# Splitting one of two fused activation sums by itself in a Strassen-style feed-forward

## The chip, the cores and the metric

The kernel runs on one core of a Trainium2 chip, in one launch. The metric is device time in microseconds (us): the median of repeated runs. A separate profiled execution gives the rows that are read here. Engines: PE (TensorE, matrix products), DVE (VectorE), ACT (ScalarE), POOL (GpSimd), SP (issues DMAs).

## The reference, cut to what matters

Two layers of a streaming encoder run over 1024 prompt tokens and 32 sample tokens (1056 columns together). The change touches only the feed-forward of each layer, D_MODEL = 1024, D_FF = 4096:

```
def channel_and_ple(h, p_i, norm_ffn_w, w_ff1, w_ff2, norm_ple_w, w_ple_gate, w_ple_proj):
    u = rms_norm(h, norm_ffn_w) @ w_ff1
    h = h + jnp.square(jax.nn.relu(u)) @ w_ff2
    ...
```

Everything else (input projections, latent attention, retention, output projection, gated embedding) is as in an ordinary encoder layer and is left out.

## The kernel before, in words

**Numbers.** Every operand of a big product is kept as a pair of 16-bit tiles, a high part and a remainder ("lo"): ACT writes the high part with a copy, DVE or POOL then subtracts it from the 32-bit source and writes the remainder. `split_ops` (around L780) does this for operands of the second half of the feed-forward: one ACT copy, one subtraction. A product is three matmuls for each block of 128 inputs: weight high by operand high, weight high by operand lo, weight lo by operand high.

**Seven products.** Tokens are halved (columns 0 to 527 and 528 to 1055) and features are paired, so that a product is a 2 by 2 block product, done in seven products after Strassen and Winograd. Products are numbered 1 to 7 and issued in the order 1, 7, 6, 4, 5, 2, 3. `PROD` says which of the seven operands (0 to 6) a product reads:

```
PROD = {1: 0, 2: 1, 3: 6, 4: 2, 5: 3, 6: 4, 7: 5}
```

So the second product issued (7) reads operand 5, the third (6) reads operand 4.

**First half** (`ff1_units`). A unit is 264 columns of each half (two units, here u0 and u1, go through each product one after the other: 12 matmuls each) of one pair of feature blocks. In the first two steps of a layer the units are 176 wide and there are three pairs. There are 34 units in each layer, 68 in all. After each product `ff1_chains` starts the work on its result. The four blocks of the activation are y11, y12, y21, y22, and the operands of the second half are 0: y11, 1: y12, 2: y22, 3: s1 = y21 + y22, 4: s2 = s1 - y11, 5: y11 - y21, 6: y12 - s2. The scratch tile Ra of a unit (named `ra` in the trace) has two quarters of the rows read here: `lo` (first) and `up` (second). y21 stands in `up`; y11 stands in PSUM (`u.f`, named `mx`); s1 stands in `rb`; y22 stands in `mm`.

**Where the change is** (`c11`, around L915). After product 2 has given y11, `c11` waits until s1 has been planned, writes y11 - y21 over `up` and s1 - y11 into `lo`, and splits both with one `split_ops` for operands (4, 5): one ACT copy and one subtraction, 528 wide (`r<-ra` on ACT, `r<-ra,r` on DVE or POOL).

**Second half** (`ff2_units`). Four steps of the first half (75 us) are followed by four steps of the second half, and so on, four times in each layer. The first step of the second half begins directly behind product 3 of the last unit. These eight places, where the second half begins, are called crossings 1 to 8 here: crossing 1 begins at about 693.5 us, crossing 2 at 850.5, crossing 3 at 1005.8, crossing 4 at 1159.7; crossings 5 to 8, in the second layer, at 2023.1, 2181.1, 2336.7 and 2490.3. The second half adds each product into h with a DVE instruction (`h<-o,h` and the like).

**Order.** A planner (`Pipe`, `Model`) fixes the order of every engine's instructions when the program is built, by a model of costs. Each chain is a generator: it hands over its next instruction, which is placed when its inputs and its engine are free in the model; among those that can go, first come goes first. A chain that waits for another (`u.has("s1")`) looks again every 0.2 us of model time. The model lets DVE instructions with two SBUF inputs and POOL instructions with SBUF inputs run only one at a time ("port"). `tt` (also inside `split_ops`) lets the planner choose DVE or POOL. On the chip the engines run their queues strictly in this order. At the same time as all this, ACT, DVE and POOL convert the next weights (`w<-s`, `w<-stage`, `w<-t` on ACT and DVE, `t<-stage,s`, `stage<-stage`, `t<-stage,t`, `t<-s,t` on POOL).

Of the kernel before, what the change touches and what calls it, by code (L numbers as in the profile page):

```python
# [15 lines left out]
ALU = mybir.AluOpType  # L16
# [157 lines left out]
def drop(*tiles):  # L174
    for t in tiles:
        if Slots.parts.get(t.name, 0) > 1:
            Slots.parts[t.name] -= 1
            continue
        slots, i = Slots.owner.pop(t.name)
        slots.free.append(i)  # L180
# [212 lines left out]
def kernel(ctx, tc, xT, pT, wts, vecs, qnw, kvnw, cf, ch, cckT, ckrT, st_in,  # L393
# [5 lines left out]
    pipe = Pipe()  # L399
# [61 lines left out]
    def tt(first, *args, bias=0.2, lead=0.3, **kw):  # L461
        other = pool if first is dve else dve
        return Either((first.q.tensor_tensor(*args, lead=lead, **kw), other.q.tensor_tensor(*args, lead=lead, **kw)), bias)

    dve, act, pool = (Engine(e, k, model, keep, ordered)
                      for e, k in ((nc.vector, "dve"), (nc.scalar, "act"), (nc.gpsimd, "pool")))
# [159 lines left out]
    def halves(a):  # L626
        return a.rearrange("p (s t) -> p s t", s=2)
# [124 lines left out]
    def split_ops(op, which, src, a, w, eng):  # L752

        if len(which) == 2:
            sl = op["p"][which]
            hi, lo = sl[:, 0, :, a:a + w], sl[:, 1, :, a:a + w]
        else:
            sl = op["o"][which[0]]
            hi, lo = sl[:, 0, a:a + w], sl[:, 1, a:a + w]
        yield act.q.activation(hi, src, AF.Copy, scale=1.0)  # L760
        yield dve.q.tensor_tensor(lo, src, hi, op=ALU.subtract) if eng is None else tt(eng, lo, src, hi, op=ALU.subtract)
        for o in which:
            op["n"][o].update(range(a // 88, (a + w) // 88))
# [78 lines left out]
    def stt(out, a, s, b, op0=ALU.mult, op1=ALU.add):  # L842
        dve.scalar_tensor_tensor(out, a, s, b, op0=op0, op1=op1)
# [26 lines left out]
    def ff1_chains(u, i, rc):  # L870
        w, op, a, Ra, Rb = u.w, u.op, u.a, u.ra, u.rb
        lo, up = Ra[:, :w], Ra[:, w:2 * w]
        e7, s1 = Rb[:, :w], Rb[:, w:2 * w]
        if i == 1:
            act.activation(lo, u.A[:, :w], AF.Copy, scale=UN)
        elif i == 7:
            act.activation(e7, u.e, AF.Copy, scale=UN)
        elif i == 6:
            act.activation(up, u.A[:, :w], AF.Copy, scale=UN)
        elif i == 4:  # L880
            stt(up, u.e, UN, up)

            def c21():
                yield dve.q.scalar_tensor_tensor(up, up, 0.0, up, op0=ALU.max, op1=ALU.mult)
                u.got.add("y21")
            pipe.spawn(c21())
        elif i == 5:
            stt(u.e, u.A[:, :w], UN, e7)

            def y22():  # L890
                yield from split_ops(op, (2,), u.e, a, w, None)
                yield u.has("s1")
                drop(u.E)

            def c22():
                yield act.q.activation(u.e, u.e, AF.Relu)
                yield act.q.activation(u.e, u.e, AF.Square)
                pipe.spawn(y22())
                yield u.has("y21")
                yield dve.q.tensor_tensor(s1, up, u.e, op=ALU.add)  # L900
                u.got.add("s1")
                yield from split_ops(op, (3,), s1, a, w, dve)
                yield u.has("s2")
                drop(Rb)
            pipe.spawn(c22())
        elif i == 2:
            stt(lo, u.f, UN, lo)
            stt(u.f, lo, 0.0, lo, ALU.max, ALU.mult)

            def y11():  # L910
                yield from split_ops(op, (0,), u.f, a, w, None)
                yield u.has("s2")
                drop(u.F)

            def c11():  # L915
                pipe.spawn(y11())
                yield u.has("s1")
                yield dve.q.tensor_tensor(up, u.f, up, op=ALU.subtract)
                yield dve.q.tensor_tensor(lo, s1, u.f, op=ALU.subtract)
                u.got.add("s2")  # L920
                yield from split_ops(op, (4, 5), halves(Ra[:, :2 * w]), a, w, dve)
                yield u.has("s4")
                drop(Ra)
            pipe.spawn(c11())
        else:
            act.activation(u.A[:, :w], u.A[:, :w], AF.Relu, scale=UN)

            def y12():
                yield from split_ops(op, (1,), u.A[:, :w], a, w, None)
                yield u.has("s4")  # L930
                drop(u.A)

            def c12():
                yield act.q.activation(u.A[:, :w], u.A[:, :w], AF.Square)
                pipe.spawn(y12())
                yield u.has("s2")
                yield dve.q.tensor_tensor(rc, u.A[:, :w], lo, op=ALU.subtract)
                u.got.add("s4")
                yield from split_ops(op, (6,), rc, a, w, pool)
                u.got.add("end")  # L940
            pipe.spawn(c12())

    def ff1_units(*units):
        pipe.wait(lambda: room(2 * len(units) + 1))
        R = T("r")
        for u in units:
            u.ra, u.rb = T("ra"), T("rb")
        for i, name, kind, start in ((1, "A", None, True), (7, "E", "mm", True), (6, "A", None, False), (4, "E", "mm", False),
                                     (5, "A", None, False), (2, "F", "mx", True), (3, "A", None, False)):
            for n, u in enumerate(units):  # L950
                u.prod(i, name, kind, start)
                ff1_chains(u, i, R[:, n * u.w:(n + 1) * u.w])
                pipe.poll()
            seen = []
            for u in units:
                if all(u.W is not x for x in seen):
                    u.done(i)
                    seen.append(u.W)

        def rest():  # L960
            yield lambda: all("end" in u.got for u in units)
            drop(R)
        pipe.spawn(rest())
# [87 lines left out]
    for L in range(DEPTH):  # L1051
# [823 lines left out]
        for e in range(4):  # L1875
# [14 lines left out]
            for z in range(4):  # L1890
                n = 8 * e + 4 + z
                load(n + 1)
                for g in range(1 if n < 31 else 3):
# [6 lines left out]
                    if e == 3 and z == 0 and g == 0:  # L1900
# [13 lines left out]
                        up = Units(upt[i // 2][:, (i % 2) * 1024:(i % 2 + 1) * 1024].rearrange("p (a n) -> p a n", a=2) for i in range(4))  # L1914
# [154 lines left out]
```

## Time and profile before

| what | value |
|---|---|
| median of 3 runs | 2712.25 us (2709.64 to 2714.51) |
| the profiled execution | 2710.96 us, its span 2709.2 us |
| mean granted TensorE clock | 0.974 of full speed |
| PE busy | 2566.6 us, 95% of the span |
| DVE busy | 1866.6 us, 69% |
| ACT busy | 1310.0 us, 48% |
| POOL busy | 1056.2 us, 39% |

The span is what the trace covers; the execution's own time has 1.8 us more around it. Busy shares are means over the whole span: the stretches in which an engine sets the pace are found in the rows of those stretches.

### The profile page before, as it was taken

How to read it: one execution, taken by the hardware profiler on the slowest of the kernel's cores; microseconds unless marked ns; L12 is line 12 of the kernel's file. 1: busy time of each engine (PE TensorE's matmuls, PEld its weight loads, DVE VectorE, ACT ScalarE, POOL GpSimd, SP SyncE). 2: the span in 40 equal slices, each digit the busy share in tenths (PEclk: the TensorE clock that was granted, in tenths of full speed). 3: DMA queues.
4: the chain of work that ended last, by engine and by line, in shares of the span. 5: the costliest groups of instructions: out<-in, count | busy, mean ns of one | idle time of the engine just before them, and what ended most of it. 6: DMA issues, size and time to landing. Idle time of an engine off the chain costs nothing.

```text
span 2709.2 us, 58534 instructions
## 1 busy us (share of the span) xinstructions
PE 2566.6 (95%) x23322; PEld 2006.0 (74%) x23322; DVE 1866.6 (69%) x4555; ACT 1310.0 (48%) x3277; POOL 1056.2 (39%) x1267
## 2 busy tenths in 40 slices
PE   7998989988999999999999989999799999999997
PEld 4765667768888888887656556777688888888965
DVE  6767776656667585875657677775585766768755
ACT  6533366646345262635445344665462534536342
POOL 7123355654333332433331334564732333333331
PEclk8999989989999999999999999999899999999999
DMA  4201010000111212121112011100011111122112
GB/s 136 71 28 49 17 53 27 21 9 33 51 60 52 67 40 75 43 68 50 56 53 70 9 41 34 58 6 29 13 40 50 57 52 59 53 66 68 56 44 64
DMA packets 87057, 130.53 MB, mean 48 GB/s; under 512 B 11584, under 2 KB 36448, under 8 KB 86784
## 3 DMA queue, kind: packets, MB, share of 16 engines
q1 hardware_dynamic: 86496, 126.25, 15.1%
q8 instruction: 182, 2.98, 0.4%
q14 instruction: 91, 0.75, 0.1%
q10 hardware_dynamic: 288, 0.55, 0.1%
HBM read 116.98 MB, written 7.02 MB: 46 GB/s over the span
## 4 chain that ended last, share of the span: by engine, by line
PE 86%; DVE 8%; POOL 3%; ACT 2%; issue 1%; DMA 0%; DVEq 0%; POOLq 0%; ACTq 0%
PE mm L476 33%; PE o L476 20%; PE st L476 19%; PE mx L476 12%; DVE r L285 3%; POOL x L285 1%; PE st L483 1%; PE mx L483 1%; DVE ra L285 1%; DVE w L285 1%; POOL r L285 1%; DVE sf L285 0%; DVE mt L285 0%; PE mm L483 0%; DVE h L285 0%
## 5 line engine op out<-in xcount | busy, mean ns | idle before, releaser
L476 PEld LDWEIGHTS <-w 128*128 128x128 f16 x13176 | 1276.5, 99 | 315.6 <-issue 50.3
L476 PE MATMUL mm<-w,x 128*128 128x256 f16 (+3 forms) x1920 | 334.9, 326 | 11.6 <-DVE sil L285 6.0
L476 PEld LDWEIGHTS <-x 128*128 128x128 f16 x2304 | 222.0, 99 | 147.7 <-DVE sil L285 10.8
L476 PE MATMUL st<-x,w 128*128 128x264 f16 (+2 forms) x1896 | 247.0, 284 | 19.1 <-ACT ra L285 19.1
L285 DVE SCALAR_TENSOR_TENSOR w<-s,w 128x512 f16<-128x512 f32 (+2 forms) x280 | 216.5, 779 | 16.5 <-ACT w L285 14.9
L476 PE MATMUL mm<-x,w 128*128 128x264 f16 (+2 forms) x1800 | 224.7, 281 | 1.3 <-DVE rb L285 1.3
L285 ACT ACTIVATE w<-t 128x512 f16<-128x512 f32 x186 | 111.0, 623 | 226.3 <-POOL t L285 224.9
L476 PE MATMUL o<-x,w 128*128 128x264 f16 (+1 forms) x1608 | 209.7, 282 | 0.0
L476 PE MATMUL mm<-r,w 128*128 128x264 f16 (+1 forms) x1584 | 189.0, 275 | 20.6 <-DVE r L285 20.6
L285 POOL TENSOR_TENSOR pp<-e,pp 128x512 f16<-128x512 f32 (+1 forms) x160 | 169.9, 1073 | 73.9 <-ACT pp L285 59.4
L476 PE MATMUL o<-r,w 128*128 128x264 f16 (+1 forms) x1584 | 196.4, 275 | 0.0
L285 POOL TENSOR_TENSOR t<-stage,s 128x512 f32<-128x512 f32 x64 | 83.8, 1310 | 279.7 <-DMA stage<-in_wts_dram 242.8
L476 PE MATMUL st<-r,w 128*128 128x264 f16 (+1 forms) x1512 | 187.7, 276 | 0.5 <-DVE r L285 0.5
L285 ACT ACTIVATE w<-s 128x512 f16<-128x512 f32 (+2 forms) x280 | 166.8, 599 | 38.3 <-DMA s<-in_wts_dram 23.6
L285 POOL TENSOR_TENSOR t<-s,t 128x512 f32<-128x512 f32 x64 | 81.6, 1275 | 264.5 <-DVE w L285 234.8
L285 ACT ACTIVATE w<-stage 128x512 f16<-128x512 f32 (+1 forms) x130 | 79.3, 613 | 175.7 <-POOL stage L285 159.0
L285 DVE SCALAR_TENSOR_TENSOR w<-t,w 128x512 f16<-128x512 f32 x186 | 135.0, 734 | 26.6 <-ACT w L285 25.4
L285 DVE SCALAR_TENSOR_TENSOR h<-mm,h 128x264 f32<-128x264 f32 (+4 forms) x184 | 82.7, 449 | 88.2 <-PE mm L476 87.4
L285 POOL TENSOR_TENSOR r<-r 128x176 f32<-128x176 f32 (+2 forms) x94 | 67.6, 729 | 154.9 <-ACT qh L285 73.0
L285 DVE SCALAR_TENSOR_TENSOR h<-o,h 128x264 f32<-128x264 f32 (+2 forms) x150 | 64.1, 429 | 91.6 <-PE o L476 90.6
L476 PE MATMUL mx<-x,w 128*128 128x264 f16 (+2 forms) x984 | 124.4, 282 | 0.8 <-DVE w L285 0.8
L476 PE MATMUL st<-qh,k 97*128 97x256 f16 (+5 forms) x672 | 123.7, 259 | 0.0
(293 smaller groups left out, 5049.6 us busy)
## 6 DMA issues: line engine op xcount, KB each, us to landing
s<-in_wts_dram SPq DMA_DIRECT2D x256, 256.0 KB
stage<-in_wts_dram SPq DMA_DIRECT2D x64, 512.0 KB
out_dram<-r SPq DMA_DIRECT2D x24, 176.0 KB
s<-in_wts_dram SPq DMA_DIRECT2D x20, 192.0 KB
h<-in_xT_dram SPq DMA_DIRECT2D x6, 512.0 KB
s<-in_wts_dram SPq DMA_DIRECT2D x16, 144.0 KB
k<-kr SPq DMA_DIRECT2D x16, 136.1 KB
out_dram<-cn SPq DMA_DIRECT2D x16, 128.0 KB
```

What stands on the lines that cost most here:

```text
L285: x = f(*args, **kw)
L476: keep(nc.tensor.matmul(out, lhsT, rhs, start=start, stop=stop, skip_group_check=skip))
L483: keep(nc.tensor.transpose(out, in_, ident))
```

## The change

y11 - y21 goes into `lo` instead of over `up`, so it no longer destroys y21 and no longer has to wait for s1; it is formed as soon as y11 and y21 are there, and a chain of its own (`s3`) splits it for operand 5 alone. When s1 is there, s1 - y11 goes over `up` and is split for operand 4 alone. y12's chain reads s2 from `up`. The scratch Ra is given back when both splits and operand 6's sum have been planned.

```diff
+            def s3():
+                yield from split_ops(op, (5,), lo, a, w, dve)
+                u.got.add("x5")
+
             def c11():
                 pipe.spawn(y11())
+                yield u.has("y21")
+                yield dve.q.tensor_tensor(lo, u.f, up, op=ALU.subtract)
+                pipe.spawn(s3())
                 yield u.has("s1")
-                yield dve.q.tensor_tensor(up, u.f, up, op=ALU.subtract)
-                yield dve.q.tensor_tensor(lo, s1, u.f, op=ALU.subtract)
+                yield dve.q.tensor_tensor(up, s1, u.f, op=ALU.subtract)
                 u.got.add("s2")
-                yield from split_ops(op, (4, 5), halves(Ra[:, :2 * w]), a, w, dve)
-                yield u.has("s4")
+                yield from split_ops(op, (4,), up, a, w, dve)
+                yield u.has("s4", "x5")
                 drop(Ra)
...
                 yield u.has("s2")
-                yield dve.q.tensor_tensor(rc, u.A[:, :w], lo, op=ALU.subtract)
+                yield dve.q.tensor_tensor(rc, u.A[:, :w], up, op=ALU.subtract)
```

## Rows read from the trace of the kernel before

**Rows 1.** The page: busy time of the engines.

```profile
PE 2566.6 (95%) x23322; PEld 2006.0 (74%) x23322; DVE 1866.6 (69%) x4555; ACT 1310.0 (48%) x3277; POOL 1056.2 (39%) x1267
```

**Rows 2.** PE's instructions that read tile r: its waits (us, times); groups by line: busy, mean ns, idle before.

```profile
  DVE r L285: 21.2, 10
...
L476 PE MATMUL mm<-r,w 128*128 128x264 f16 x1440 | 175.8, 279 | 20.6 <-DVE r L285 20.6
```

**Rows 3.** Timeline, crossing 2: start, duration, engine, instruction, idle before it and releaser.

```profile
847.06 0.44 DVE L285 SCALAR_TENSOR_TENSOR mx<-ra 128x264 f32<-128x264 f32 x1
...
849.27 0.42 DVE L285 SCALAR_TENSOR_TENSOR ra<-ra 128x264 f32<-128x264 f32 x1
849.39 0.39 ACT L285 ACTIVATE r<-mx 128x264 f16<-128x264 f32 x1 [1.09 <-DVE mx L285]
...
849.95 0.42 DVE L285 TENSOR_TENSOR ra<-mx,ra 128x264 f32<-128x264 f32 x1
850.28 1.29 POOL L285 TENSOR_TENSOR t<-stage,s 128x512 f32<-128x512 f32 x1 [1.23 <-DMA stage<-in_wts_dram]
...
850.63 0.42 DVE L285 TENSOR_TENSOR r<-mx,r 128x264 f16<-128x264 f32 x1
...
853.15 1.29 PE L476 MATMUL mm<-r,w 128*128 128x264 f16 x10
...
855.04 1.68 DVE L285 TENSOR_TENSOR r<-ra,r 128x528 f16<-128x528 f32 x1
...
856.77 3.14 PE L476 MATMUL mm<-r,w 128*128 128x264 f16 x14 [2.34 <-DVE r L285]
```

**Rows 4.** Stretches: length, busy (instructions) of PE, PEld, DVE, ACT, POOL, granted clock, DMA.

```profile
703.00:709.00 6.00, 6.00 (x41) 4.62 (x39) 3.20 (x7) 1.89 (x4) 0.00 (x0) 0.72 0.00 0
...
850.00:857.00 7.00, 4.66 (x42) 3.92 (x40) 6.72 (x16) 5.49 (x14) 6.64 (x6) 0.99 0.00 0
857.00:865.00 8.00, 8.00 (x59) 6.31 (x57) 4.25 (x9) 1.02 (x2) 1.54 (x2) 0.79 0.15 35
...
2032.40:2040.00 7.60, 7.60 (x44) 5.61 (x44) 3.55 (x8) 2.11 (x5) 0.00 (x0) 0.64 0.00 0
...
2187.60:2196.00 8.40, 8.35 (x60) 6.65 (x60) 4.39 (x9) 1.15 (x3) 1.81 (x2) 0.80 0.10 33
```

**Rows 5.** PE: timeline of crossing 2, product 2 before and after it; undisturbed piece of the chain.

```profile
845.05 2.86 PE L476 MATMUL mx<-x,w 128*128 128x264 f16 x24
...
868.11 2.86 PE L476 MATMUL mx<-r,w 128*128 128x264 f16 x24
...
1041.01 2.70 PE mx L476 x24
```

**Rows 6.** Groups by line and form: the fused split and the single splits.

```profile
L285 DVE TENSOR_TENSOR r<-ra,r 128x528 f16<-128x528 f32 x50 | 53.7, 1083 | 0.4 <-ACT r L285 0.4
...
L285 ACT ACTIVATE r<-ra 128x528 f16<-128x528 f32 x56 | 35.7, 638 | 7.4 <-DVE ra L285 7.4
...
L285 ACT ACTIVATE r<-rb 128x264 f16<-128x264 f32 x56 | 23.4, 418 | 1.3 <-DVE rb L285 0.4
...
L285 DVE TENSOR_TENSOR r<-rb,r 128x264 f16<-128x264 f32 x36 | 17.3, 479 | 0.0
...
L285 POOL TENSOR_TENSOR r<-rb,r 128x264 f16<-128x264 f32 x20 | 13.7, 687 | 125.6 <-ACT r L285 125.6
```

**Rows 7.** Stretch of four steps of the first half, columns as in rows 4.

```profile
923.00:1001.00 78.00, 78.00 (x696) 67.83 (x694) 59.39 (x122) 45.31 (x114) 28.17 (x24) 1.00 0.17 55
```

**Rows 8.** Timeline, crossing 1.

```profile
697.06 0.64 ACT L285 ACTIVATE r<-ra 128x528 f16<-128x528 f32 x1 [0.66 <-DVE ra L285]
...
698.65 0.82 DVE L285 SCALAR_TENSOR_TENSOR w<-s,w 128x512 f16<-128x512 f32 x1
...
700.94 1.76 DVE L285 TENSOR_TENSOR r<-ra,r 128x528 f16<-128x528 f32 x1
...
702.76 0.39 PE L476 MATMUL mm<-r,w 128*128 128x264 f16 x2 [3.50 <-DVE r L285]
```

## The prediction

> **What bounds the kernel now.** I read the page first: PE is busy for 95% of the span [rows 1], so time is won only where PE stands still or runs slowly. Next came PE's waits by tile. The operand tiles of the second half, r, cost PE 21.2 us in ten waits, and 20.6 of them stand before the matmuls into bank mm [rows 2]. In the second half the only matmuls into mm that begin a step are those of product 7, which reads operand 5, one of the two sums that the change separates. Eight of the ten waits are one for each crossing; the other two, 0.5 us together, are at product 1 of crossings 1 and 5. Then I read the timelines of the crossings, and last the granted clock around them.
>
> The reader is to see three things. First, in crossing 2, PE does ten matmuls of product 7 for u0 and stops until 856.77, when a 528-wide subtraction on DVE, begun at 855.04, has ended [rows 3]. Nine matmuls are the first three blocks; the tenth takes the high part of the newest block, the eleventh its remainder. So PE waits for the remainder of operand 5 alone, and that is made in one instruction with the remainder of operand 4, which PE reads a whole product later. Second, DVE is full there: busy 6.72 of 7.00 us [rows 4]. It isn't waiting for anything; the operand comes late because of the order of DVE's queue and the width of the instruction. Third, the clock: after four of the waits PE ran below full speed, at means of 0.72, 0.79, 0.64 and 0.80 over 6.0, 8.0, 7.6 and 8.4 us [rows 4], a mixture of its two levels, 1.2 and 2.4 GHz; behind the other four crossings it stayed at 2.4 GHz.
>
> **What there is to win.** Waits: 21.2 us. Slow clock: 6.0 x 0.28 + 8.0 x 0.21 + 7.6 x 0.36 + 8.4 x 0.20 = 1.7 + 1.7 + 2.7 + 1.7 = 7.8 us. A stop also costs a little at its end. From product 2 before crossing 2 to product 2 behind it is 868.11 - 845.05 = 23.06 us; without a stop it would be seven products for two units at 2.70, 18.9 [rows 5]. Of the loss of 4.16 the wait is 2.34 [rows 3] and the slow clock 1.7; 0.1 is left, eight times that is 1.0. Together 30.0 us is all that the crossings lose, and the most that I let the change win.
>
> **The change, part by part.** *Removed:* in each of 68 units one ACT copy of 528 and one subtraction of 528, and the wait of y11 - y21 for s1. *Added:* two copies and two subtractions of 264. ACT: 2 x 0.418 - 0.638 = +0.20 us for a unit [rows 6], 13 us in all at most (12 of the units are narrower). DVE: 2 x 0.479 - 1.083 = -0.13 us by the means, since both are partly held up by POOL; at most, all on POOL, 2 x 0.687 = 1.37 against 1.083. What hides it: in four steps of the first half PE is busy 78.0 of 78.0 us, ACT 45.3, DVE 59.4, POOL 28.2 [rows 7]; eight units add 1.6 us to ACT and under 2.4 to the others. I cost it at nothing there. If that cover were gone it would be the 13 us. No DMA is added or moved past another step in SP's queue.
>
> *Moved, u0.* y11 of u0 is written at 847.06 [rows 3], and its y21 has long been there. Today y11 - y21 comes at 849.95, because its chain asks for s1 again 0.2 us later and then stands behind u1's steps. After the change it can be placed directly after y11, behind s1 at the latest: by about 847.8. ACT has nothing to do for 1.09 us before 849.39 [rows 3], so the copy fits there, done by about 848.8. The remainder then goes to DVE between its other steps (849.95 and 850.63 are two steps apart, so 0.34 us each) or to POOL, which stands idle for 1.23 us before 850.28 [rows 3]. Done by 849.7 at best. If it lands behind the first of POOL's three weight subtractions, 851.6 + 0.7 = 852.3; behind all three, which end at 850.28 + 3 x 1.3 = 854.2, at 855.0. PE wants it at 853.15 + 1.29 = 854.4. So: no wait in all cases but the last, and 0.6 in that.
>
> *Moved, u1.* Its y21 is finished only at 849.27 + 0.42 [rows 3]; y11 - y21 follows some four DVE steps later, 851.2, the copy by about 852.4, the remainder at 853 to 855.0. PE wants it 1.35 us after u0's, at 855.7. No wait.
>
> *Operand 4.* s1 - y11 keeps its place. Its remainders are wanted at 853.15 + 2.70 + 1.12 = 857.0 for u0 and 858.3 for u1. Today the last of this group, 528 wide, ends at 855.04 + 1.68 = 856.72 [rows 3]. DVE's and POOL's work up to there stays as large (above), and the two additions into h that come earlier when PE doesn't stop add 0.7: 857.4 at worst, a wait of 0 to 0.4.
>
> *Crossings 1 and 5* lose most, because u1's copy, ready at 697.70, finds weight subtractions (from 698.65 on) ahead of its own subtraction at 700.94 [rows 8]. There operand 5 of u1 will be ready before 697, wanted at 699. Operand 4 may stay behind the weights: 700.94 + 0.42 to 702, against 701.5 wanted: up to 0.6 us.
>
> *Product 1* reads y11, whose remainder for u0 comes at 850.63 to 851.05 [rows 3], only some 0.5 us before PE's eleventh matmul of that product. A subtraction that is put ahead of it costs 0.34 and is covered; two are not: 0.2 us at a crossing as a guess between 0 and 0.5. The same order may put s1, which frees bank mm, 0.3 us later in the first pair of each layer, where PE already waits for it.
>
> *Sum of what stays:* six crossings x 0.3 + two x 0.6 + eight x 0.2 + two x 0.3 = 1.8 + 1.2 + 1.6 + 0.6 = 5.2 us. None of these waits is long compared with those after which the clock stayed up, so I leave no slow clock. Gain 30.0 - 5.2 = 24.8 us. The profiled execution's 2710.96 (span 2709.2 and 1.8 around it) becomes 2686.2; the median of the runs is 1.3 higher, so I say **2687 us**.
>
> **A rule that speaks against it.** The DVE is busy 6.72 of 7.00 us in crossing 2 [rows 4], and this change gives it more and smaller instructions. The Trainium skill, "Perfetto Trace Analysis", section "Optimizing Scalar/DVE Operations", says that larger, grouped operations help a saturated engine, and in the same section that breaking instructions up may let work finish sooner where Scalar and Vector cause bubbles on another engine without being saturated. By its first sentence, with DVE saturated at the crossings, the change would lose time, in the milder form under rival (c); by the second it wins as I forecast. I follow the order of need: what PE waits for is half of the wide instruction, and the half it doesn't need yet may come 2.70 us later.
>
> **The rivals.** *(a) Main case:* above, 2680 to 2694. *(b) The wait goes half to another operand:* the planner puts the remainder of operand 5 behind POOL's weight subtractions, or operand 4 and operand 0 come late, so that 1 to 2 us stay at each crossing and at some of them the slow clock too. For it: the first place is taken by whoever comes first in the model, and POOL's three weight steps hold the port for 3.9 us. Against it: 2.70 us of product 7 stand between the two needs. 30.0 - 8 x 1.8 - 2 = about 14 us won: 2694 to 2706. *(c) Slower:* the smaller subtractions queue behind the three weight subtractions at all crossings, as 528-wide ones do at crossings 1 and 5. There the wait is 3.50 [rows 8] where it is 2.34 in crossing 2. If operand 5 came some 2 us later than now (698.65 to 700.94, less one step of 0.34) at the six other crossings, that is 12 us, and up to four more slow stretches of 1.7: +12 to +18, 2724 to 2730. It decides from the point where u1's copy for operand 5 ends after the weights' copies in ACT's queue; today it ends before them, and the change makes it earlier, so I give it little. A milder form is that the full DVE merely ends later, by 0.2 us (the surplus on ACT) for each of the 16 units at the crossings and with nothing won: +3 us, which can't be told from no change and is counted under (d). *(d) No change:* operand 5 is planned early but the queue's order leaves its subtraction where it was, or gains at the crossings are given back in the layers' other stages, whose planned order may move with the new times (norms, gate, second layer's attention): 2707 to 2718.
>
> **How the numbers follow.** Chances: (a) 0.66, (b) 0.16, (d) 0.08, (c) 0.10. A measurement of this kernel tells about 0.2%, 5.4 us, from no change. Faster by more: (a) and (b), 0.82. Within: 0.08. Slower: 0.10. The low end is the whole loss gone and the spread of the runs, 2712.25 - 30.0 - 2 = 2680; the high end reaches through most of (b), 2703; that leaves out (c), (d) and the edges of (a) and (b), about 0.2.
>
> **What would show it.** Right: PE's waits for r fall from 21.2 to below 6 us; the granted clock behind the crossings is 1.00; the copy `r<-ra` is 264 wide 112 times and 176 wide 24 times, and comes before the copy of y12 in crossing 2; DVE's span from product 2 to the last split is as long as now. Wrong: a wait before the bank o or st matmuls of product 6 or 1 as long as the one that went; 264-wide subtractions behind `w<-t`; PE losing time away from the eight crossings.

## The result: slower, and the profile after

The changed kernel takes 2730.73 us (2727.73 to 2732.79, 4 runs) beside 2711.86 us before (2709.64 to 2714.51, 4 runs on the same chip): a ratio of 1.0068, with an interval of 1.0051 to 1.0086. The forecast was 2687 and faster. The profiled execution spans 2726.0 us, 16.8 more than before, at a mean granted clock of 0.972.

The page after; the lines answer to [rows 1] and to the group of [rows 2].

```profile
PE 2568.1 (94%) x23322; PEld 2006.8 (74%) x23322; DVE 1865.0 (68%) x4599; ACT 1316.9 (48%) x3345; POOL 1058.5 (39%) x1291
...
L476 PE MATMUL mm<-r,w 128*128 128x264 f16 (+1 forms) x1584 | 187.3, 274 | 29.5 <-DVE r L285 29.5
...
L476 PE MATMUL o<-r,w 128*128 128x264 f16 (+1 forms) x1512 | 193.7, 279 | 4.4 <-DVE r L285 4.4
```

All PE waits for tile r after, as in [rows 2] (us, times):

```profile
  DVE r L285: 33.9, 15
```

No engine has much more to do: DVE 1.6 us less, ACT 6.9 more, POOL 2.3 more. But PE's waits for r grew from 21.2 us in ten to 33.9 in 15. Eight of them, 3.61 to 3.84 us each, still stand before bank mm, that is before product 7 and operand 5; seven new ones of 0.31 to 0.83 stand before bank o, in product 1.

Crossing 2 after, timeline, beside [rows 3]:

```profile
845.58 2.86 PE L476 MATMUL mx<-x,w 128*128 128x264 f16 x24
...
850.48 0.42 DVE L285 TENSOR_TENSOR ra<-mx,ra 128x264 f32<-128x264 f32 x1
850.93 0.42 ACT L285 ACTIVATE r<-ra 128x264 f16<-128x264 f32 x1
...
851.63 0.82 DVE L285 TENSOR_TENSOR r<-ra,r 128x264 f16<-128x264 f32 x1
851.84 0.61 ACT L285 ACTIVATE w<-s 128x512 f16<-128x512 f32 x1
...
852.71 0.42 DVE L285 TENSOR_TENSOR ra<-mx,ra 128x264 f32<-128x264 f32 x1
...
853.77 0.72 ACT L285 ACTIVATE r<-ra 128x264 f16<-128x264 f32 x2
...
854.33 0.39 PE L476 MATMUL o<-r,w 128*128 128x264 f16 x2 [0.71 <-DVE r L285]
...
854.55 2.64 PE L476 MATMUL mm<-r,w 128*128 128x264 f16 x22
...
856.00 0.61 ACT L285 ACTIVATE w<-stage 128x512 f16<-128x512 f32 x1
856.06 1.79 POOL L285 TENSOR_TENSOR r<-r,r 128x264 f16<-128x264 f32 x2
...
856.45 0.85 DVE L285 SCALAR_TENSOR_TENSOR w<-s,w 128x512 f16<-128x512 f32 x1
...
857.23 1.17 DVE L285 SCALAR_TENSOR_TENSOR w<-stage,w 128x512 f16<-128x512 f32 x1
...
858.33 0.68 DVE L285 SCALAR_TENSOR_TENSOR w<-t,w 128x512 f16<-128x512 f32 x1
...
858.93 1.83 DVE L285 TENSOR_TENSOR r<-ra,r 128x264 f16<-128x264 f32 x2
859.08 1.39 POOL L285 TENSOR_TENSOR t<-s,t 128x512 f32<-128x512 f32 x1 [1.23 <-DVE w L285]
...
860.81 0.39 PE L476 MATMUL mm<-r,w 128*128 128x264 f16 x2 [3.62 <-DVE r L285]
861.03 2.56 PE L476 MATMUL st<-r,w 128*128 128x264 f16 x12
```

Read it in two halves. For u0 the outcome is the one forecast, but not through an earlier sum: y11 - y21 comes 4.90 us after the start of product 2 (850.48 - 845.58), exactly as before (849.95 - 845.05, [rows 3] and [rows 5]). What is earlier is its copy, 850.93, which needn't wait for operand 4's sum any more, and with it the remainder, 851.63; PE runs 22 matmuls of product 7 without a stop (12 of u0, 10 of u1). For u1 the sum comes at 852.71 and its copy, the first of the two that begin at 853.77, is done by 854.2, but the remainder is the second of the two subtractions that begin at 858.93, behind all three weight subtractions, and the pair takes 1.83 us beside POOL's `t<-s,t`; PE stands still for 3.62 us. In [rows 3] the stop was 2.34, and the tenth matmul was u0's. This is the picture that before showed at crossings 1 and 5 alone [rows 8]; now all eight crossings have it.

The granted clock behind three of the stops, columns as in [rows 4]:

```profile
861.00:869.00 8.00, 8.00 (x59) 6.31 (x57) 3.95 (x9) 2.21 (x5) 0.00 (x0) 0.79 0.01 3
1018.50:1026.00 7.50, 7.50 (x54) 5.93 (x53) 3.61 (x8) 2.71 (x5) 0.72 (x1) 0.78 0.00 1
...
2040.40:2048.00 7.60, 7.60 (x46) 5.55 (x45) 2.65 (x6) 1.97 (x4) 0.00 (x0) 0.65 0.00 0
```

Taken over 8.0 us from the end of the stop, such rows give 0.64 to 0.83 behind all eight crossings. Their length times what is missing to 1.00 is 14.2 us; before it was 7.8, at four crossings.

**Where the time went.** A crossing's loss is the time from product 2 before it to product 2 behind it, less 18.9 us, as in the prediction. After, the eight losses are 5.67, 6.32, 6.14, 6.13, 7.07, 6.45, 6.39 and 6.10, together 50.27 us; before 30.44. So the crossings cost 19.8 us more: 12.7 of longer stops, 6.4 of slow clock, 0.7 of the rest. The span grew by 16.8, so elsewhere it is 3.0 us shorter; that is no more than two profiled executions can differ by without a change (see e5).

### The profile page after: what moved, and what is told of

Same layout as the page of the kernel before. It is cut to its first block, busy times and chain, and to the rows that moved or that the text cites. A ratio compares the mean times of both kernels' runs of the same rounds, so it can differ in the third digit from the quotient of the medians.

```text
span 2726.0 us, 58694 instructions
## 1 busy us (share of the span) xinstructions
PE 2568.1 (94%) x23322; PEld 2006.8 (74%) x23322; DVE 1865.0 (68%) x4599; ACT 1316.9 (48%) x3345; POOL 1058.5 (39%) x1291
## 4 chain that ended last, share of the span: by engine, by line
PE 87%; DVE 8%; POOL 2%; ACT 2%; issue 1%; DMA 0%; SPq 0%; DVEq 0%; POOLq 0%; ACTq 0%
PE mm L476 33%; PE o L476 20%; PE st L476 19%; PE mx L476 12%; DVE r L285 2%; DVE w L285 1%; PE st L483 1%; POOL x L285 1%; PE mx L483 1%; POOL r L285 1%; DVE ra L285 1%; DVE sf L285 0%; DVE mt L285 0%; PE mm L483 0%; ACT w L285 0%
## 5 line engine op out<-in xcount | busy, mean ns | idle before, releaser
L476 PE MATMUL st<-x,w 128*128 128x264 f16 (+2 forms) x1800 | 229.5, 280 | 19.0 <-ACT ra L285 19.0
L476 PE MATMUL o<-x,w 128*128 128x264 f16 (+1 forms) x1704 | 228.6, 287 | 0.0
L285 DVE SCALAR_TENSOR_TENSOR w<-s,w 128x512 f16<-128x512 f32 (+2 forms) x280 | 211.4, 760 | 16.2 <-ACT w L285 14.8
L476 PE MATMUL st<-r,w 128*128 128x264 f16 (+1 forms) x1584 | 204.0, 281 | 0.0
L285 DVE SCALAR_TENSOR_TENSOR w<-t,w 128x512 f16<-128x512 f32 x186 | 132.3, 719 | 20.2 <-ACT w L285 19.9
```

The source lines that it names most:

```text
L285: x = f(*args, **kw)
L476: keep(nc.tensor.matmul(out, lhsT, rhs, start=start, stop=stop, skip_group_check=skip))
```

## The experiments

**The theory** is that of rival (c): the remainder of operand 5 is placed behind the three weight subtractions. In the order that the planner fixes, POOL's weight steps hold the model's port until u1's remainder is ready to go as well; when the port comes free, the weights' chain has waited longest, and a chain that has just placed a step hands over its next at once, so its three DVE subtractions go in a row (e8 changes just this). Against it stands that the change gives full engines more and smaller instructions and that these, not the place, make the loss. In the expectations Q stands for the theory of the queue's place and L for the rival. Each kernel ran beside the kernel before on the same chip: runs e1 to e4 beside 2713.34, e5 to e8 beside 2710.86, e9 and e10, on another chip, beside 2712.03 us.

### Each half of the change alone (e3, e4)

e3 keeps the order of sums of before and splits operands 5 and 4 separately:

```diff
+            def s3():
+                yield from split_ops(op, (5,), up, a, w, dve)
+                u.got.add("x5")
...
                 yield dve.q.tensor_tensor(up, u.f, up, op=ALU.subtract)
+                pipe.spawn(s3())
                 yield dve.q.tensor_tensor(lo, s1, u.f, op=ALU.subtract)
-                yield from split_ops(op, (4, 5), halves(Ra[:, :2 * w]), a, w, dve)
+                yield from split_ops(op, (4,), lo, a, w, dve)
...
```

> The kernel before with the split alone: the sums stay where they were and wait for s1, the scratch isn't swapped, but operands 5 and 4 are split by themselves. In the order as built the three weight subtractions stand ahead of u1's remainder at all crossings, as in the changed kernel. Theory Q: as slow as the changed kernel, 2724 to 2738, waits of 3.4 us and more at product 7 of all crossings. Rival S (the early sum is what costs, by pushing other steps back): as the kernel before, 2707 to 2717.

e4 has the early sum and the swapped scratch, but one split 528 wide (for that the pair's order in its tile is turned round); its diff is against the changed kernel:

```diff
-    PAIRS_R = ((0, 1), (2, 3), (4, 5), (6,))
+    PAIRS_R = ((0, 1), (2, 3), (5, 4), (6,))
...
-                pipe.spawn(s3())
                 yield u.has("s1")
                 yield dve.q.tensor_tensor(up, s1, u.f, op=ALU.subtract)
...
-                yield from split_ops(op, (4,), up, a, w, dve)
+                yield from split_ops(op, (5, 4), halves(Ra[:, :2 * w]), a, w, dve)
```

> The kernel before with the early sum and the swapped scratch, but both operands still split by one copy and one subtraction of 528 (the pair's order in its tile is swapped for that). In the order as built the three weight subtractions stand ahead of the fused subtractions at all crossings. Theory Q: product 7 waits for the remainder of u0 already, 4 us and more at all crossings; slower than the kernel before, 2722 to 2742. Rival F (the two smaller instructions are what costs): as the kernel before, 2707 to 2717.

Measured: e3 2733.22 us (ratio 1.0072, 1.0056 to 1.0088), e4 2746.16 us (1.0121, 1.0104 to 1.0138). Crossing 2 of e3:

```profile
858.58 1.09 DVE L285 SCALAR_TENSOR_TENSOR w<-s,w 128x512 f16<-128x512 f32 x1
...
860.69 0.68 DVE L285 SCALAR_TENSOR_TENSOR w<-t,w 128x512 f16<-128x512 f32 x1
861.29 1.83 DVE L285 TENSOR_TENSOR r<-ra,r 128x264 f16<-128x264 f32 x2
...
863.17 0.60 PE L476 MATMUL mm<-r,w 128*128 128x264 f16 x2 [4.66 <-DVE r L285]
```

Crossing 2 of e4:

```profile
858.65 1.25 DVE L285 SCALAR_TENSOR_TENSOR w<-s,w 128x512 f16<-128x512 f32 x1
...
861.42 1.17 DVE L285 SCALAR_TENSOR_TENSOR w<-t,w 128x512 f16<-128x512 f32 x1
862.86 1.76 DVE L285 TENSOR_TENSOR r<-ra,r 128x528 f16<-128x528 f32 x1
...
864.67 3.24 PE L476 MATMUL mm<-r,w 128*128 128x264 f16 x14 [5.86 <-DVE r L285]
```

Either half alone brings the same picture at every crossing: stops of 4.4 to 5.0 us in e3 (37.5 in eight), of 5.8 to 6.3 in e4 (47.1 in eight). e4 was expected at 2722 to 2742 and came out above: as expected it is already u0's remainder that stands behind the weights there, but the stops, put at 4 us and more, are 5.8 to 6.3. e4 has no additional small instructions, so their number isn't what costs; and without its other half each half loses at least as much as the whole change.

### The weights' subtractions held back (e1, e2, e6)

```diff
     def split_ops(op, which, src, a, w, eng):
+        mark = 4 in which or 5 in which
+        due[0] += mark
         ...
+        due[0] -= mark
...
     def put(W, i, src):
         yield act.q.activation(w[:, 0], src, AF.Copy, scale=SW)
+        yield lambda: due[0] == 0
         yield dve.q.scalar_tensor_tensor(w[:, 1], src, SW, w[:, 0], op0=ALU.mult, op1=ALU.subtract)
```

A weight's subtraction is planned only when no split for operand 4 or 5 is under way. e1 has this on the changed kernel, e2 on the kernel before, e6 on the changed one, in the last step ahead of each crossing alone.

> The changed kernel, with one addition: a weight's subtraction on DVE is not planned while a split for operand 4 or 5 has begun and not ended. In the order as built, the remainders of operands 4 and 5 then stand ahead of the three weight subtractions at every crossing. Theory Q (the queue): the 3.6 us waits at product 7 come from these three subtractions standing ahead of u1's remainder; with them behind it, that wait falls to 0.5 to 1 us at each crossing, the sum of PE's waits for r falls from 33.9 to under 15 us, and the median to 2690 to 2702, below both kernels. Rival L (late anyway): the remainder of u1 is late through its own chain (y21, ACT's copy, a full DVE), whatever stands ahead; the wait at product 7 stays above 2 us and the median at 2720 to 2731. Rival W (weights): the wait at product 7 goes, but PE then waits for weights as long: 2715 to 2730.

> The kernel before with the same addition. Theory Q: only crossings 1 and 5 had the weight subtractions ahead, so only they gain: they lose some 3 us each instead of 5.8 and 6.8; the six others stay at 2 to 4; in all 5 to 7 us, median 2704 to 2709. Rival L: no change, 2709 to 2716. Rival W: slower by what the later weights cost, 2715 to 2725.

> The changed kernel with the hold of e1, but only for the splits of the last step ahead of each crossing; in the sixteen or so steps between, weights and splits stand in the order the planner gives. Theory Q: the crossings lose 12 to 17 us together as in e1, and the median is 2690 to 2700. Rival E (e1 won mostly elsewhere, since the hold also reorders the other steps): the crossings lose less but the median stays at 2705 or above.

Measured: e1 2692.24 us (0.9922, 0.9906 to 0.9938); e2 2698.76 (0.9947, 0.9932 to 0.9962); e6 2694.14 (0.9938, 0.9922 to 0.9955). Crossing 2 of e1:

```profile
854.50 1.46 DVE L285 TENSOR_TENSOR r<-ra,r 128x264 f16<-128x264 f32 x2
...
856.01 0.39 PE L476 MATMUL mm<-r,w 128*128 128x264 f16 x2 [0.78 <-DVE r L285]
856.24 1.51 PE L476 MATMUL st<-r,w 128*128 128x264 f16 x12
...
858.13 0.68 DVE L285 SCALAR_TENSOR_TENSOR w<-s,w 128x512 f16<-128x512 f32 x1
...
860.44 1.27 POOL L285 TENSOR_TENSOR t<-s,t 128x512 f32<-128x512 f32 x1 [4.77 <-DVE w L285]
```

The same two subtractions now come before the weights, the stop at product 7 is 0.78 instead of 3.62, and the product behind it takes 1.51 us, full speed, instead of 2.56. The eight crossings lose 13.6 us instead of 50.3. e6 loses 14.7 there and takes 1.9 us more than e1 by the medians, inside the spread of their runs: what matters is the place at the crossings, not the order elsewhere. e2 was expected at 2704 to 2709 and won more: 8.8 us at the crossings (30.4 to 21.7) and 5.3 of its span elsewhere. Between e2 and e1, both with the weights out of the way, lies what the change itself is worth: 6.5 us by the medians; at the crossings it is 8.0 (21.7 to 13.6).

### The place alone, forced on the kernel before (e5)

```diff
         yield act.q.activation(hi, src, AF.Copy, scale=1.0)
+        if op.get("last", False) and 5 in which and a:
+            seen = put_n[0]
+            yield lambda: put_n[0] >= seen + 3
         yield dve.q.tensor_tensor(lo, src, hi, op=ALU.subtract) if eng is None else ...
...
         yield dve.q.scalar_tensor_tensor(w[:, 1], src, SW, w[:, 0], op0=ALU.mult, op1=ALU.subtract)
+        put_n[0] += 1
...
+                    rr[-1]["last"] = z == 2
```

At the crossings u1's fused remainder is planned only after three more weight subtractions; all else is as before.

> The kernel before, without the change, with one wait added in the planner: at the crossings alone, the fused remainder of u1 for operands 4 and 5 is placed only after three more weight subtractions. In the order as built they now stand ahead of it at crossings 2 to 4 and 6 to 8 as they already did at 1 and 5; the sums, the copies and their widths are those of the kernel before. Theory Q: this alone makes the slowness: a second wait of 2.5 to 4 us at product 7 at each of the six crossings, with slow clock 3 to 4 us each, +15 to +24 us, median 2727 to 2738. Rival L (three subtractions ahead cost only their own 2 us and PE covers them with product 7 of u0): 2712 to 2720.

Measured: 2719.91 us (2715.91 to 2728.83, 6 runs), 1.0035 (1.002 to 1.005): slower, but half as much as the theory asked, and inside the range of its rival. Crossing 2 of e5, and the clock behind it and behind crossing 6:

```profile
860.06 1.51 PE L476 MATMUL mm<-r,w 128*128 128x264 f16 x12 [1.52 <-DVE r L285]
...
862.04 0.69 DVE L285 SCALAR_TENSOR_TENSOR w<-t,w 128x512 f16<-128x512 f32 x1
862.64 0.70 DVE L285 TENSOR_TENSOR r<-ra,r 128x528 f16<-128x528 f32 x1
862.80 1.67 POOL L285 TENSOR_TENSOR t<-s,t 128x512 f32<-128x512 f32 x1 [2.25 <-DVE w L285]
863.39 0.39 PE L476 MATMUL mm<-r,w 128*128 128x264 f16 x2 [1.82 <-DVE r L285]
```

```profile
863.40:871.00 7.60, 7.60 (x68) 6.62 (x68) 4.90 (x10) 2.71 (x5) 1.07 (x1) 1.00 0.21 71
...
2195.00:2203.00 8.00, 7.69 (x52) 5.92 (x52) 4.39 (x10) 2.71 (x5) 1.38 (x1) 0.74 0.15 36
```

The stop of 1.82 us behind `w<-t` is there as forced; it is as long at five of the six crossings and 0.83 at crossing 6, where 2.5 to 4 were expected. u0's remainder still comes first, so PE stops twice, 1.52 and 1.82 us with 12 matmuls between, where the changed kernel stops once for 3.62. At this crossing the sum is nearly the same; but the clock behind crossings 2, 3, 4, 7 and 8 stays at 1.00, where the changed kernel lost 1.4 to 1.7 us each time, and the new stop at product 1 (0.71 in crossing 2) is missing.

The eight crossings of e5 lose 36.8 us, 6.4 more than before, where those of the changed kernel lose 19.8 more. The 9.1 us by the medians (2719.91 - 2710.86) hold more than that: e5's profiled span is 9.4 us longer, and 4.1 of these lie ahead of product 2 before crossing 1 (692.2 against 688.1 us), up to where both kernels run the same instructions in the same order. So the place by itself costs about a third of what the change lost at the crossings. The rest comes with the form that it takes in the changed kernel, one long stop with slow clock behind it and the stop at product 1; e5 doesn't have this form, and for it the evidence is e1, e6 and e8, where the weights are moved away.

### The stop at product 1, and a simpler remedy (e7, e8, e9, e10)

e7 is e1 with y11's remainder allowed to be planned further ahead (a lead of 0.7 instead of 0.3 us; the lead is how long before it is ready, in the model, an instruction may be given its place); e8 is the changed kernel with one line, which sends the weights' chain to the back of the planner's line after its copy; e9 has that line in the kernel before; e10 has the lead of e7 and the line of e8.

```diff
-                yield from split_ops(op, (0,), u.f, a, w, None)
+                yield from split_ops(op, (0,), u.f, a, w, None, 0.7)
```

```diff
     def put(W, i, src):
         yield act.q.activation(w[:, 0], src, AF.Copy, scale=SW)
+        yield 0.25
         yield dve.q.scalar_tensor_tensor(w[:, 1], src, SW, w[:, 0], op0=ALU.mult, op1=ALU.subtract)
```

> e1 with a second addition: the remainder of y11 (operand 0) may be placed up to 0.7 us early in DVE's queue, since e1 and the changed kernel both have a new wait of 0.3 to 1.0 us at product 1 for it. Theory Q: that wait goes (5.2 us in all), the one at product 7 stays under 1 us: 2683 to 2692. Rival M (the wait only moves: something else of the full DVE is then late by as much): 2690 to 2700.

> The changed kernel with another remedy: after each ACT copy a weight's chain waits 0.25 us of model time before it asks for its subtraction, so that it goes to the back of the line and not ahead of chains that were waiting. Nothing is held for a split. In the order as built the three weight subtractions stand behind all four remainders of operands 4 and 5 at the crossings. Theory Q with the planner's line as its cause: the waits at product 7 fall under 1.5 us each, median 2690 to 2706. Rival (the delays cost the weights more than the splits win): 2710 or more.

> The kernel before, in which the weights' chain steps to the back of the planner's line after its ACT copy, as in the run of the changed kernel that took 2683.6. Theory (the change by itself, with the weights out of the way, is worth what the earlier arrival of operand 5 at the crossings saves): the planned order has the fused remainders ahead of the weights at all eight crossings, so each crossing loses about as much as in the run of before with the hold (2.3 to 4.3 us, 21.7 in all), PE waits some 15 us for r before mm, and the time is 2692 to 2702; the change is then worth 9 to 18 us on top. Rival (the remedy does everything and the change adds nothing): 2681 to 2687.

> The changed kernel with the weights' chain at the back of the line, and y11's remainders with a lead of 0.7 us instead of 0.3. If the waits of 1.1 to 2.2 us at product 1 that were left (11.8 us in 8) are due to y11's remainder standing behind the subtractions for operand 5, they go and the time is 2673 to 2681. Rival: the lead moves a weight subtraction ahead of them (the planned order shows one at every crossing) and the waits stay or are moved to operand 4: 2682 to 2692.

Measured: e7 2685.58 us (0.9911, 0.9896 to 0.9925), e8 2683.64 (0.9901, 0.9886 to 0.9916), e9 2697.42 (0.995, 0.9935 to 0.9966), e10 2707.14 (0.999, 0.998 to 1.0).

e7: the stops at product 1 are gone from all eight crossings, and with short ones elsewhere (0.44 to 0.77 before operand 4 at six crossings) the loss there falls from 13.6 to 8.4. e8 came out below its range: the weights go behind operands 5 and 4 here too, and what is left at crossing 2 is one stop at product 1:

```profile
850.78 0.39 PE L476 MATMUL o<-r,w 128*128 128x264 f16 x2 [2.20 <-DVE r L285]
...
854.49 1.41 DVE L285 TENSOR_TENSOR r<-ra,r 128x264 f16<-128x264 f32 x2
...
856.17 0.67 DVE L285 SCALAR_TENSOR_TENSOR w<-s,w 128x512 f16<-128x512 f32 x1
```

Its crossings lose 14.8 us, no less than e1's; it wins the rest elsewhere. e9 came in its range, with 29.0 us lost at the crossings where 21.7 were expected. Against e9 the change is worth 13.8 us by the medians, or 12.6 if each is taken against the kernel before on its own chip; at the crossings it is 14.2 (29.0 to 14.8). What the line itself wins elsewhere is the same in both: from product 2 behind crossing 4 to product 2 before crossing 5 e8 and e9 take 835.4 us (842.8 before), and from product 2 behind crossing 8 to the end 197.6 and 197.3 (202.8 before). e7 and e8 both beat the kernel before and the changed kernel.

e10 missed both of its cases. PE, crossing 2 of e10:

```profile
851.55 1.51 PE L476 MATMUL o<-r,w 128*128 128x264 f16 x12
852.90 1.51 PE L476 MATMUL st<-r,w 128*128 128x264 f16 x12
854.25 2.91 PE L476 MATMUL mm<-r,w 128*128 128x264 f16 x24
```

Here is the crossing of the forecast: no stop at all, a loss of 0.04 to 0.05 us at six crossings, 9.2 over all eight. And yet e10 spans 2704.0 us, 21.8 more than e8. From product 2 behind crossing 4 to product 2 before crossing 5 it takes 847.9 us where e8 takes 835.5, and from product 2 behind crossing 8 to the end 211.3 against 197.6. The waits in that last piece, PE's timeline, and the clock behind them:

```profile
2573.60 1.59 PE L476 MATMUL mm<-diag,ones 128*128 128x128 f32 x6 [3.17 <-ACT diag L285]
2585.17 6.15 PE L476 MATMUL mm<-x,w 128*128 128x352 f16 x22 [5.13 <-DVE w L285]
```

```profile
2573.70:2577.00 3.30, 3.30 (x13) 2.33 (x14) 1.78 (x5) 2.20 (x6) 1.51 (x3) 0.50 0.00 0
2585.20:2590.60 5.40, 5.40 (x19) 2.82 (x20) 3.26 (x5) 0.63 (x1) 1.15 (x1) 0.50 0.42 113
```

Behind the second half, PE stops 3.17 us for a result of ACT and 5.13 for a weight's remainder, and behind each stop it runs at half speed, for 3.3 and 5.4 us: 3.2 + 5.1 + 4.4 = 12.7 us. The same stops, 3.17 and 5.13, stand behind crossing 4. e8, which differs by the lead alone, has stops of 0.37 and 0.35 us in their place and a clock of 1.00; less these, 11.9 of the 13.7 us are accounted for. So the longer lead, which frees the crossings, makes a weight and a norm late in the next stage; by what steps of the planner was not followed.

## Why the prediction was wrong

**What failed** is "Moved, u1", with its "the remainder at 853 to 855.0 ... No wait". I worked out from when the operand could be ready, and let DVE take it up some steps later. The sum came 1.5 us later than I had it (852.71 against 851.2; 0.5 of it because product 2 itself began at 845.58 and not at 845.05), the copy ended 1.8 later (854.2 against 852.4), and that alone would have been in time for PE, which wants the remainder at 854.55 + 2.64 = 857.2. But the queue's next free place went to the weights, and the remainder ended at 860.8. e1, e6 and e8 take the weights out of the way by two different edits, and the stop at product 7 falls to 0.57 to 1.26 us or, at six crossings of e8, goes; e5 puts them in the way and a stop of 1.82 comes. The same holds for the sentence on crossings 1 and 5: there, too, "ready before 697" didn't mean written before 697, and the stop grew from 3.50 to 3.84 at crossing 1 and to 3.61 at crossing 5.

**Rival (c)** named the mechanism, its sign and nearly its price (2724 to 2730 against 2730.73). The price is in part luck: it counted 12 us more of stops at product 7 of six crossings, which are 8.4, and nothing at product 1, which is 3.9 more than before; its slow clock, up to 6.8, is 6.4. I gave it 0.10 on a condition that doesn't decide: whether u1's copy ends after the weights' copies in ACT's queue. In crossing 2 it ends by 854.2; only one weight's copy, `w<-s` at 851.84, comes ahead of it, `w<-stage` begins at 856.00, and the subtraction goes behind all three all the same. [Rows 8] showed before that a split that was ready early stood behind weights; I took the late copy for its cause.

**The slow clock** was sized at nothing because I expected short stops; it is 14.2 us. **Product 1** was a guess of 0.2 us a crossing, between 0 and 0.5; it is 0.31 to 0.83 at seven crossings, 4.4 us, and e7 shows whose order it is: y11's remainder.

**What held:** PE's loss at the crossings does come from the order of DVE's queue (e1, e6). u0's remainder was in time, though not by the way in "Moved, u0": the sum, which I had by 847.8 once it needn't wait for s1, came at 850.48, as long after product 2 as before, so s1 wasn't what held it. That is the same mistake as with u1, at a place where it cost nothing. The cover in the first half held: from product 2 behind a crossing to product 2 before the next, both kernels take 132.3 us at all six such places, and ACT has 6.9 us more work in all, under my bound of 13. A single 264-wide subtraction on DVE costs more, by the mean, than the 0.479 that I took: with 96 on DVE at a mean of 0.707 and 16 on POOL at 0.742, two of them are some 1.4 us against 1.083 for the wide one, my upper bound; DVE's total is lower all the same.

**The size of the win** was too large also with the weights out of the way: 6.5 us (e2 to e1) and 13.8 (e9 to e8) where 24.8 were forecast. Part of the 30 us belongs to the place of the weights, which the change doesn't touch (8.8 at the crossings in e2), and e10, with six crossings free of stops, shows that what is won there can be lost again later in the layer.

The Trainium skill, "Perfetto Trace Analysis", section "Optimizing Scalar/DVE Operations", says that grouped operations help a saturated engine, and that breaking instructions up may let work finish sooner where the engine isn't saturated but causes bubbles on others. The traces agree with the sign of the first (e3, the smaller instructions alone, is 19.9 us slower), but not through DVE's load, which is 1865.0 us after and 1866.6 before; and e4, which keeps the grouped instruction, is 32.8 slower. With the weights out of the way they agree with the second (6.5 us from e2 to e1, 13.8 from e9 to e8), although DVE is about as full as it was (busy 1876.8 us in e1, 1850.8 in e8).

What stays open: by which steps e2, e8 and e9 win several us away from the crossings (in e8 and e9 alike, so not by the change), and at which stops the clock falls (below).

## What to carry to other kernels

When an order is fixed by list scheduling, an instruction that becomes ready earlier isn't thereby placed earlier: look at what else has been waiting for the same engine or port, and for how long, before taking a readiness time as a start time. If one place of the trace already shows the bad order (here crossings 1 and 5), ask what keeps the other places from it, and forecast both outcomes until that is known. Before splitting a fused step, move the work that it would queue behind, and then look for what that makes late, in the whole layer.

## What the hardware showed that was not expected

The length of PE's stop doesn't tell whether the granted clock falls behind it. Stops of 3.6 us and more were followed by the lower level every time (all eight crossings after). Below that both happen: before, 2.34 us was followed by it and 2.47 was not; in e9 a stop of 2.15 us at crossing 8 was followed by 0.79 over 8.0 us, one of 2.19 at crossing 7 by 1.00 (the two rows below, columns as in [rows 4]); in e5 two stops of 1.52 and 1.82 left it at 1.00, and two of 2.06 and 0.83 were followed by 0.74.

```profile
2489.00:2497.00 8.00, 8.00 (x57) 6.33 (x57) 4.67 (x10) 3.12 (x6) 1.27 (x1) 0.79 0.22 54
2334.90:2343.00 8.10, 8.09 (x72) 7.04 (x72) 6.08 (x12) 2.71 (x5) 1.28 (x1) 1.00 0.13 32
```

A DVE instruction's time depends on what POOL does beside it. The 128x512 weight subtraction takes 0.68 us in e1, where POOL is idle beside it, and 1.17 after, at 857.23, beside POOL's two subtractions of 128x264; the 128x528 split takes 1.68 in [rows 3], with POOL at work, and 0.70 in e5 at 862.64, where it began 0.16 us ahead of POOL's next subtraction of 128x512; that one then took 1.67 us, and 1.27 in e1 at 860.44. I had taken the mean over all of them, 1.083, for a price.
